# Earlier loads in the branch projections, and splits, loads and sums dealt anew around W_o, its norms and the first gate pair

## The chip, the cores and the metric

The kernel runs on one core of a Trainium2 chip. The time is that of one execution on the device, in microseconds (us), as the median of several runs. The engines are called PE (TensorE, matrix products), DVE (VectorE), ACT (ScalarE), POOL (GpSimd) and SP (SyncE, which issues most of the DMA transfers).

## The reference, cut to what matters

One layer of a decoder for a prompt of 1024 tokens and 8 single tokens of other sequences (1032 columns in all), with 1024 channels in float32:

```python
h = _rmsnorm(x, lp['norm1_w']) * (1 + sc1) + sh1
qkv, gdn_gate, beta_raw, a_raw, sq, sk, sv, ga, gb = _split_in(h @ lp['w_in'])
...
y_a = _gdn_out(o_a, gdn_gate, lp['gdn_onorm_w']) @ lp['w_gdn_out']
...
y_b = o_b @ lp['w_swa_out']
mix = (jax.nn.sigmoid(ga) * y_a + jax.nn.sigmoid(gb) * y_b) @ lp['w_o']
x = x + gt1 * mix
h2 = _rmsnorm(x, lp['norm2_w']) * (1 + sc2) + sh2
gate = h2 @ lp['w_ffn_gate']
up = h2 @ lp['w_ffn_up']
...
gc = _causal_dwconv(gate_ext, lp['ffn_conv_w'], L) + lp['ffn_conv_b']
x = x + gt2 * ((jax.nn.silu(gc) * up) @ lp['w_ffn_down'])
```

The part that is touched here begins with the two output projections of the branches, `w_swa_out` and `w_gdn_out`, goes on with `w_o` and the second norm, and ends in the first pair of blocks of `w_ffn_gate`.

## The kernel before

Every product of float32 matrices is made of three matmuls of rounded numbers. An operand x is split into a high part, x rounded by ACT (`split`, L129), and a low part, x minus the high part, made on DVE (L130); `mm3` adds high by high (L180), low by high (L181) and high by low (L182). A weight or an activation is ready for PE when both engines are done with it; the first of the three matmuls needs only the high parts. A block of 128 output channels takes 24 matmuls for each group of columns.

The work is kept transposed, channels on the 128 partitions and tokens along the free axis. In the branches the tokens are cut into three parts (`PARTS`: t = 0, 1 of 384 columns, t = 2 of 264), from W_o on into four quarters (`QUARTERS`, q = 0 to 3, of 256 to 260).

`branches` (L1332) first runs y_b: for each block j of 128 channels of `w_swa_out` the product of `ob`, times its gate (`yb_out`). While it does so, `oa` and the part of y_b that was parked in DRAM (`ub`) are loaded, at j = 3 and 4 (L1364). Then it runs y_a with `w_gdn_out`: `ya_out` (L1343) multiplies by the gate, adds y_b and splits the sum into the operands of W_o, `self.mix` (tiles `bmh`, `bml`). Beside these products stands the recurrence of the 8 single tokens (`sample_delta`), whose states go through DRAM (`dlr`) into `b1l`, are scaled by ACT (L1216) and updated by DVE.

`output_pass` (L1407) makes quarter q of W_o: for each j the weight (`output_weights`, only at q = 0, with three `raw` buffers), the residual x from DRAM (`xT`, L1431), the product, the addition on DVE (L1472) and the square for the norm; the sum is also written to `x1d`. The room of x is that of operands of the last branch product, so its loads can start only once that product is done. `second_norm` (L1479) sums the squares on PE, takes the power -1/2 on POOL (`power`, L125), spreads the factors with a diagonal `dg` (DVE, L1505) and a matmul (PE, L1506), and scales.

The feed-forward products run in a form in which a pair of blocks takes seven products in place of eight: `operands` makes sums and differences of the columns (tiles `bmh`, `pk`, differences in `td`), `pair_weights` (L1577) those of the weights (`ws`, on POOL for `w_ffn_gate`), and `ffn_gate_up` runs the pair.

The code gives streams of instructions with priorities (`weave`); a scheduler, which models the time of each instruction, puts each engine's instructions in one order, and each engine takes them strictly in that order. `issue_after` keeps what follows behind a given instruction. Since SP is one such engine, a transfer that waits for its room holds back all behind it.

Of the kernel before, what the change touches and what calls it, by code (L numbers as in the profile page):

```python
# [64 lines left out]
class Step:  # L65
# [57 lines left out]
    def power(self, out, in_, expo):  # L123
        e = expo[:in_.shape[0], :]
        self.nc.gpsimd.tensor_tensor(out, in_, e.broadcast_to(list(in_.shape)), op=ALU.pow)  # L125

    def split(self, hi, lo, x, eng=None):

        self.nc.scalar.activation(hi, x, AF.Copy)  # L129
        (eng or self.nc.vector).tensor_tensor(lo, x, hi.bitcast(F32), op=ALU.subtract)  # L130
# [1201 lines left out]
    def branches(self, pool, pool2):  # L1332
# [10 lines left out]
        def ya_out(t, ps):  # L1343
            u, v = ub[t][:, j, :], gate(self.sga, j, t)
            nc.vector.tensor_tensor(v, ps, v, op=ALU.mult)
            nc.vector.tensor_tensor(u, u, v, op=ALU.add)
            r0, n = PARTS[t]
            for q, (lo, m) in enumerate(QUARTERS):
                c, e = max(lo, r0), min(lo + m, r0 + n)
                if c < e:  # L1350
                    self.split(*(x[:, j, c - lo:e - lo] for x in self.mix[q]), u[:, c - r0:e - r0])
# [4 lines left out]
        for j, t in (*late[:2], *((j, t) for j in range(7) for t in (0, 1) if t or (j, t) in late[2:]), (7, 1), *late[-1:] * (7 not in EARLY)):  # L1356
# [7 lines left out]
            if t and j in (3, 4):  # L1364
                with self.tc.issue_after(self.w_load.ins):
                    if j == 3:
# [40 lines left out]
    def output_pass(self, pool, q):  # L1407
# [5 lines left out]
        def add(t, ps):  # L1413
            self.add_gated(t, ps, j, 16)
            sq = self.t(pool, [P, QW], "nsq" if j else "nss", bufs=2)[:, :n]
            if q == 3 and j > 4:
                nc.vector.tensor_tensor(sq, x1[:, j, :], x1[:, j, :], op=ALU.mult)
            else:
                nc.scalar.activation(sq, x1[:, j, :], AF.Square)
# [8 lines left out]
        for j in range(8):  # L1428
            if q == 0:
                self.wo.append(self.output_weights(j))  # L1430
            nc.sync.dma_start(x1[:, j, :], self.xT[j][:, lo:lo + n])  # L1431
# [12 lines left out]
    def output_weights(self, j):  # L1444
# [9 lines left out]
        for c in (0, 512) if j == 0 else (slice(None),):  # L1454
            c = c if j else slice(c, c + 512)
            self.split(*(x[:, c] for x in w), raw[:, c])
# [22 lines left out]
    def second_norm(self, pool, psum, t):  # L1479
# [22 lines left out]
        self.power(rs[:, :nc_], rs[:, :nc_], self.mhalf)  # L1502
# [18 lines left out]
    def operands(self, pool, p, stage):  # L1521
# [21 lines left out]
        self.split(*ops[2], d)  # L1543
        yield
        minus(b1, b2, b1)
        self.split(*ops[4], b1)
        yield
        minus(a2, a2, d)
        self.split(*ops[5], a2)
        yield  # L1550
        self.split(*ops[6], b2)
# [25 lines left out]
    def pair_weights(self, pool, w, f, eng=None):  # L1577
# [20 lines left out]
        out = [put(a0), put(b0)]  # L1598
        s1 = calc(a1, b1, ALU.add)
# [53 lines left out]
    def ffn_gate_up(self, pool, pool2, psum, f, w, first):  # L1653
# [9 lines left out]
        def gate(p, i, q, ps, r):  # L1663
            lo, n = QUARTERS[2 * p + q]
            zq = z[i][:, 2 + lo:2 + lo + n]
            if r is None:
                nc.scalar.copy(zq, ps)
            else:
                nc.vector.tensor_tensor(zq, ps, r, op=ALU.add)
# [25 lines left out]
        w = self.pair_weights(pool, I["w_ffn_up"][0], f, nc.vector if first else None)  # L1695
# [213 lines left out]
    def second_half(self):  # L1909

        nc, S = self.nc, ExitStack
        with S() as c:
# [6 lines left out]
            with S() as right:  # L1919
                xr = self.pool("xr", 1, ctx=right, side="right")  # L1920
                with S() as left:
# [3 lines left out]
                    self.squares, self.X, self.wo = {}, {}, []  # L1925
# [151 lines left out]
```

## Time and profile before

| | |
|---|---|
| runs | 2074.53, 2076.88, 2081.3 us, median 2076.88 |
| profiled execution | 2076.01 us |
| its span in the profile | 2074.3 us |
| PE busy | 2008.0 us, 97% of the span |
| DVE, ACT, POOL busy | 1356.4, 902.5, 522.1 us |
| moved by DMA | 275.75 MB, 133 GB/s over the span |

A profile row gives the start in us from the span's beginning, the duration, engine and line of the kernel (a helper's line where one records the operation), the output and inputs by their tile names, and in brackets how long the engine had been idle before it and what released it. SPq rows are transfers that SP issues: their duration is that of the issue. PE rows of one form overlap, so that the step from start to start tells the speed. Stretches of time show, for each engine, busy time, then the granted clock of PE, the mean use of the DMA engines and the bytes moved.

### The profile page before, as it was taken

Reading aid. Unit: us, or ns where it says so; the run is one execution under the profiler, and the core shown is the slowest. Engines: PE = TensorE matmul, PEld = TensorE weight load, DVE = VectorE, ACT = ScalarE, POOL = GpSimd, SP = SyncE. Lnnn points to the kernel's source line nnn. Section 1 sums busy time; section 2 is a strip of 40 time slices with the busy share of each in tenths; the row PEclk is TensorE's granted clock in tenths of the full one; section 3 lists DMA queues with packets and bytes.
Section 4 is the critical chain, followed back from the end, with each engine's and each line's share of the span. In section 5 each row is a group of like instructions: output and inputs, shape, how many; then the busy total and the mean of one; then the engine's idle time right before and its main releaser. Section 6 shows DMA issues by size and latency. Waiting matters only on the chain.

```text
span 2074.3 us, 41298 instructions
## 1 busy us (share of the span) xinstructions
PE 2008.0 (97%) x16245; PEld 1905.2 (92%) x16245; DVE 1356.4 (65%) x2714; ACT 902.5 (44%) x2233; POOL 522.1 (25%) x594
## 2 busy tenths in 40 slices
PE   7999999999999999989989999999999999999998
PEld 4987877799999999979989999999999999999997
DVE  4755767483655746656554575479886777668866
ACT  4664545443334343442442452345544444444443
POOL 2000000131321211211111000004556556543561
PEclk9999999999999999999999999999999999999999
DMA  8256443332322322312276774513333332388783
GB/s 293 72 145 207 138 168 116 96 99 65 82 82 57 77 69 52 91 37 61 67 198 184 253 231 133 146 58 90 105 98 103 107 95 91 126 280 280 265 285 115
DMA packets 301887, 275.75 MB, mean 133 GB/s; under 512 B 59730, under 2 KB 248111, under 8 KB 301676
## 3 DMA queue, kind: packets, MB, share of 16 engines
q1 hardware_dynamic: 295642, 252.14, 39.7%
q0 software_dynamic: 5552, 20.37, 2.8%
q8 instruction: 127, 2.08, 0.4%
q14 instruction: 68, 0.56, 0.1%
q10 hardware_dynamic: 498, 0.61, 0.1%
HBM read 212.93 MB, written 62.51 MB: 133 GB/s over the span
## 4 chain that ended last, share of the span: by engine, by line
PE 82%; DMA 6%; DVE 6%; ACT 3%; issue 1%; SPq 1%; POOL 0%; DVEq 0%; POOLq 0%; ACTq 0%
PE mm L180 18%; PE mm L181 18%; PE mm L182 18%; PE wv L180 3%; PE wv L182 3%; PE wv L181 3%; PE wy L182 2%; PE wy L180 2%; PE wy L181 2%; PE pv L652 1%; DMA raw<-in_w_swa_out_dram 1%; PE pt L190 1%; PE tp L190 1%; PE mm L264 1%; PE sc L614 1%
## 5 line engine op out<-in xcount | busy, mean ns | idle before, releaser
L180 PE MATMUL mm<-b1h,wh 128*128 128x384 f32 (+1 forms) x1520 | 496.9, 328 | 4.0 <-ACT gt L1294 1.6
L181 PE MATMUL mm<-b1l,wh 128*128 128x384 f32 (+1 forms) x1520 | 489.1, 323 | 0.0
L182 PE MATMUL mm<-b1h,wl 128*128 128x384 f32 (+1 forms) x1520 | 487.7, 323 | 0.4 <-DVE wl L130 0.3
L180 PEld LDWEIGHTS mm<-b1h,wh 128*128 128x128 f32 x1520 | 286.5, 189 | 13.1 <-issue 4.6
L181 PEld LDWEIGHTS mm<-b1l,wh 128*128 128x128 f32 x1520 | 286.8, 189 | 4.4 <-issue 4.0
L182 PEld LDWEIGHTS mm<-b1h,wl 128*128 128x128 f32 x1520 | 286.0, 188 | 4.5 <-issue 2.8
L129 ACT ACTIVATE wh<-raw 128x1024 fp32r<-128x1024 f32 x83 | 87.1, 1050 | 124.4 <-PE mm L181 72.0
L130 DVE TENSOR_TENSOR wl<-raw,wh 128x1024 fp32r<-128x1024 f32 x82 | 101.9, 1244 | 59.8 <-ACT wh L129 58.9
L181 PE MATMUL mm<-pk,w 128*128 128x260 f32 (+1 forms) x440 | 124.3, 283 | 1.1 <-DVE pk L130 1.1
L180 PE MATMUL mm<-pk,w 128*128 128x260 f32 (+1 forms) x440 | 124.3, 283 | 0.0
L182 PE MATMUL mm<-pk,w 128*128 128x260 f32 (+1 forms) x440 | 124.1, 282 | 0.0
L130 DVE TENSOR_TENSOR w<-ws,w 128x512 fp32r<-128x512 f32 x88 | 78.2, 890 | 36.0 <-ACT w L129 35.8
L1626 ACT COPY bml<-mm 128x256 f32<-128x256 f32 (+1 forms) x132 | 48.9, 371 | 97.6 <-PE mm L182 94.5
L180 PE MATMUL mm<-bmh,w 128*128 128x260 f32 (+1 forms) x320 | 90.3, 282 | 0.0
L182 PE MATMUL mm<-bmh,w 128*128 128x260 f32 (+1 forms) x320 | 90.1, 282 | 0.0
L1681 DVE SCALAR_TENSOR_TENSOR fa<-fz,fcw,fa 128x512 f32<-128x512 f32 x88 | 74.5, 867 | 18.1 <-ACT fa L1679 17.8
L180 PE MATMUL mm<-b2h,wh 128*128 128x384 f32 (+1 forms) x256 | 83.2, 328 | 3.0 <-ACT wh L129 2.9
L181 PEld LDWEIGHTS mm<-pk,w 128*128 128x128 f32 x440 | 82.8, 188 | 1.3 <-DVE pk L130 1.3
L181 PE MATMUL mm<-b2l,wh 128*128 128x384 f32 (+1 forms) x256 | 83.6, 327 | 0.4 <-DVE b2l L130 0.4
L180 PEld LDWEIGHTS mm<-pk,w 128*128 128x128 f32 x440 | 82.9, 188 | 0.2 <-ACT bml L1626 0.2
L182 PEld LDWEIGHTS mm<-pk,w 128*128 128x128 f32 x440 | 82.9, 189 | 0.0
L182 PE MATMUL mm<-b2h,wl 128*128 128x384 f32 (+1 forms) x256 | 82.9, 326 | 0.0
(645 smaller groups left out, 5889.9 us busy)
## 6 DMA issues: line engine op xcount, KB each, us to landing
raw<-in_w_in_dram SPq DMA_DIRECT2D x59, 512.0 KB
ws<-in_w_ffn_down_dram SPq DMA_DIRECT2D x55, 256.0 KB
raw<-xd SPq DMA_DIRECT2D x47, 258.0 KB
raw<-in_w_ffn_down_dram SPq DMA_DIRECT2D x47, 256.0 KB
raw<-in_w_ffn_gate_dram SPq DMA_DIRECT2D x22, 512.0 KB
raw<-in_w_ffn_up_dram SPq DMA_DIRECT2D x22, 512.0 KB
qst<-in_w_mod_dram SPq DMA_DIRECT2D x16, 512.0 KB
raw<-in_w_mod_dram SPq DMA_DIRECT2D x16, 512.0 KB
```

What stands on the lines that cost most here:

```text
L129: self.nc.scalar.activation(hi, x, AF.Copy)
L130: (eng or self.nc.vector).tensor_tensor(lo, x, hi.bitcast(F32), op=ALU.subtract)
L180: mm(ps, whi, xhi, start=first, stop=False, **kw)
L181: mm(ps, whi, xlo, start=False, stop=False, **kw)
L182: self.last_mm = mm(ps, wlo, xhi, start=False, stop=last, **kw).ins
L190: self.nc.tensor.transpose(out, in_, self.ident[:p, :p])
L264: nc.tensor.matmul(ps[32 * j:32 * j + 32], self.cT[:, k0 + j, :], ws[j // 2][:, j % 2, :], start=k0 == 0, stop=k0 > 0)
L614: self.scored = nc.tensor.matmul(sc[:, r, 256 - w:256], q, KH[:, lo:lo + w], start=True, stop=False)
L652: nc.tensor.matmul(pv[64 * r:64 * r + 64], V[:, n - back, ch], ps[:, r::2, :], start=back == 0, stop=back == (n > 0))
L1626: self.last_copy = nc.scalar.copy(r[p, i], x[p])
L1681: nc.vector.scalar_tensor_tensor(ai[:, c:e], zi[:, j + c:j + e], col(j), ai[:, c:e], op0=ALU.mult, op1=ALU.add)
```

## The change

1. In `branches` the loads of `oa` part 0 and of `ub` are placed at j = 1 and 2 in place of 3 and 4.
2. `ya_out` of the last part (t = 2) for j = 6 and 7 rounds the high parts on DVE, as an addition that writes the rounded type, and no more on ACT.
3. The residual x for W_o is loaded two blocks of channels at a time: 16 transfers in place of 32.
4. The low parts of the weights j = 0 and 1 of W_o are made on POOL in place of DVE.
5. The sums of the first weight of `w_ffn_gate` are issued behind the power of the norm of quarter 1.
6. In the first gate pair, the first copy out of PSUM is DVE's in place of ACT's, the additions of its first half are issued behind the last square, and the splits of the operands and of one weight behind the split of the third operand.

```diff
     def split(self, hi, lo, x, eng=None):
-        self.nc.scalar.activation(hi, x, AF.Copy)
-        (eng or self.nc.vector).tensor_tensor(lo, x, hi.bitcast(F32), op=ALU.subtract)
+        return (self.nc.scalar.activation(hi, x, AF.Copy),
+                (eng or self.nc.vector).tensor_tensor(lo, x, hi.bitcast(F32), op=ALU.subtract))
+    def behind(self, made):
+        stack = ExitStack()
+        for x in made:
+            stack.enter_context(self.tc.issue_after(x.ins))
+        return stack
...
+            if t < 2 or j < 6:
+                nc.vector.tensor_tensor(u, u, v, op=ALU.add)
+                for rooms, a, b, m in spans:
+                    self.split(*(x[:, j, a:a + m] for x in rooms), u[:, b:b + m])
+                return
+            for (hi, _), a, b, m in spans:
+                nc.vector.tensor_tensor(hi[:, j, a:a + m], u[:, b:b + m], v[:, b:b + m], op=ALU.add)
             nc.vector.tensor_tensor(u, u, v, op=ALU.add)
+            for (hi, lo), a, b, m in spans:
+                nc.vector.tensor_tensor(lo[:, j, a:a + m], u[:, b:b + m], hi[:, j, a:a + m].bitcast(F32), op=ALU.subtract)
...
-            if t and j in (3, 4):
+            if t and j in (1, 2):
                 with self.tc.issue_after(self.w_load.ins):
-                    if j == 3:
+                    if j == 1:
                         oa = {0: self.load_part(pool2, self.oa, 0, rooms=first)}
...
-            nc.sync.dma_start(x1[:, j, :], self.xT[j][:, lo:lo + n])
+            if j % 2 == 0:
+                nc.sync.dma_start(x1[:, j:j + 2, :], self.xT[j:j + 2, :, lo:lo + n].rearrange("k p n -> p k n"))
...
-            self.split(*(x[:, c] for x in w), raw[:, c])
+            self.split(*(x[:, c] for x in w), raw[:, c], None if j > 1 else self.nc.gpsimd)
...
-        self.power(rs[:, :nc_], rs[:, :nc_], self.mhalf)
+        self.factors.append(self.power(rs[:, :nc_], rs[:, :nc_], self.mhalf))
...
-        self.split(*ops[2], d)
+        made = self.split(*ops[2], d)
         yield
-        minus(b1, b2, b1)
-        self.split(*ops[4], b1)
+        self.third = made if p else ()
+        with self.behind(self.third):
+            minus(b1, b2, b1)
+            self.split(*ops[4], b1)
...
-        out = [put(a0), put(b0)]
-        s1 = calc(a1, b1, ALU.add)
+        out = [put(a0)]
+        with self.behind(after):
+            out.append(put(b0))
+        with self.behind(self.factors[1:2] if f == 0 and len(self.factors) == 3 else ()):
+            s1 = calc(a1, b1, ALU.add)
...
-                nc.scalar.copy(zq, ps)
+                (nc.vector.tensor_copy if first and not p else nc.scalar.copy)(zq, ps)
```

How the orders change at the three places of which the prediction speaks most. SP at the start of W_o, before: `raw` are the weights of W_o (the first three of eight stand ahead of these rows), `x` the residual.

```order
L1448 DMA raw_14410<-in_w_o_dram 128x8x128
L1431 DMA x_2196_14333<-xT_950 128x256 x6
L1448 DMA raw_14447<-in_w_o_dram 128x8x128
L1431 DMA x_2196_14333<-xT_950 128x256 x3
L1448 DMA raw_14483<-in_w_o_dram 128x8x128
L1431 DMA x_2196_14333<-xT_950 128x256 x2
L1448 DMA raw_14519<-in_w_o_dram 128x8x128
```

And SP there with the change:

```order
L1464 DMA raw_14409<-in_w_o_dram 128x8x128
L1447 DMA x_2196_14333<-xT_950 128x2x256 x8
L1464 DMA raw_14446<-in_w_o_dram 128x8x128
L1447 DMA x_2197_14334<-xT_950 128x2x260 x4
L1464 DMA raw_14481<-in_w_o_dram 128x8x128
L1464 DMA raw_14517<-in_w_o_dram 128x8x128
```

Weight 3 stands behind eight transfers of two blocks in place of six of one, weight 4 behind four more of two blocks in place of three of one.

SP where the second weight of W_gdn_out is loaded, before: `oa` is the other operand, whose remaining parts are loaded into `b2l`, `dlr` the states of the recurrence, `sga` a gate.

```order
L135 DMA raw_13464<-in_w_gdn_out_dram 128x8x128
L1250 DMA b2l_2110_13423<-oa_927 128x2x256 x2
L1393 DMA gt_13419<-sgb_2613 128x384
L1250 DMA b2l_2110_13423<-oa_927 128x2x256 x2
L1214 DMA b1l_2052_12734<-dlr_13089 128x1024
L1393 DMA gt_13501<-sga_2614 128x384
L1214 DMA b1l_2052_12734<-dlr_13089 128x1024
L135 DMA raw_13470<-in_w_gdn_out_dram 128x8x128
L1250 DMA b2l_2112_13439<-oa_927 128x2x384 x4
```

And with the change:

```order
L142 DMA raw_13464<-in_w_gdn_out_dram 128x8x128
L1221 DMA b1l_2052_12734<-dlr_13089 128x1024
L1408 DMA gt_13419<-sgb_2613 128x384
L1257 DMA b2l_2110_13423<-oa_927 128x2x256 x3
L1221 DMA b1l_2052_12734<-dlr_13089 128x1024
L1257 DMA b2l_2110_13423<-oa_927 128x2x256
L1408 DMA gt_13501<-sga_2614 128x384
L1221 DMA b1l_2052_12734<-dlr_13089 128x1024
L1257 DMA b2l_2112_13439<-oa_927 128x2x384 x4
L142 DMA raw_13470<-in_w_gdn_out_dram 128x8x128
```

The states' loads have moved up, and the second weight (`raw_13470`) has gone from ahead of the last four `oa` loads to behind them. On PE the second product of W_gdn_out is now that of those four loads; before it came after those of the second weight and of part 2.

POOL at the second norm, before: `rs` are the powers of the norms of quarters 0 and 1, `ws` the sums of the first gate weight.

```order
L1589 TENSOR_TENSOR ws_15523<-raw_15513,raw_15515 128x512
L1589 TENSOR_TENSOR ws_15525<-ws_15523,raw_15513 128x512
L1589 TENSOR_TENSOR ws_15533<-raw_15513 128x512
L125 TENSOR_TENSOR rs_15396<-rs_15396,mhalf 128x2
L125 TENSOR_TENSOR rs_15431<-rs_15431,mhalf 128x2
```

And with the change:

```order
L130 TENSOR_TENSOR w_2201_14339<-raw_14336,w_2200_14338 128x512 x2
L130 TENSOR_TENSOR pk_2205_14376<-raw_14374,pk_2205_14376 128x1024
L125 TENSOR_TENSOR rs_15380<-rs_15380,mhalf 128x2
L125 TENSOR_TENSOR rs_15415<-rs_15415,mhalf 128x2
L1609 TENSOR_TENSOR ws_15507<-raw_15497,raw_15499 128x512
L1609 TENSOR_TENSOR ws_15509<-ws_15507,raw_15497 128x512
L1609 TENSOR_TENSOR ws_15517<-raw_15497 128x512
```

The low parts of W_o's first two weights are new on POOL, and both powers have moved ahead of the sums.

29 lines of the change are left out of this document (15 added, 14 removed).

## The prediction

> **What bounds the kernel now.** Read in this order: the page's busy times, whom TensorE (PE) waited for, PE's timeline at the longest of those waits, then the other engines and SP's DMA issues (SPq) there. The page first:
>
> ```profile
> PE 2008.0 (97%) x16245; PEld 1905.2 (92%) x16245; DVE 1356.4 (65%) x2714; ACT 902.5 (44%) x2233; POOL 522.1 (25%) x594
> ```
>
> PE is busy for 97% of the span, so the change, which leaves every product as it is, can only win PE's waits, and the time a low clock costs behind them. PE's waits from 1100 to 1440 us, the stretch that the edits touch (total, times, longest):
>
> ```profile
> core 0 of [0], span 2074.3 us
> engine line waited for: us in total, times, longest us
> PE nr L1506 <- DVE dg L1505: 3.0, 1, 3.0
> PE mm L180 <- ACT wh L129: 2.9, 1, 2.9
> PE mm L1439 <- ACT w L129: 2.1, 1, 2.1
> PE wv L180 <- ACT w L129: 1.1, 1, 1.1
> PE mm L181 <- DVE pk L130: 1.1, 1, 1.1
> ```
>
> The places, in order of time: **A**, the second W_gdn_out weight (2.9); **B**, the start of W_o (2.1); **C**, the norm of quarter 0 (3.0); **D**, the first gate pair (1.1 and 1.1). PE's own timeline (start, duration, instruction, idle before):
>
> ```profile
> 1195.54 0.44 PE L180 MATMUL mm<-b2h,wh 128*128 128x384 f32 x1 [2.88 <-ACT wh L129]
> ...
> 1196.36 0.38 PE L180 MATMUL mm<-b2h,wh 128*128 128x264 f32 x1
> ...
> 1199.62 0.38 PE L180 MATMUL mm<-b2h,wh 128*128 128x264 f32 x1
> ```
> ```profile
> 1285.02 0.49 PE L1439 MATMUL mm<-bmh,w 128*128 128x256 f32 x1 [2.06 <-ACT w L129]
> ...
> 1288.52 1.13 PE L1439 MATMUL mm<-bmh,w 128*128 128x256 f32 x8
> 1289.48 0.28 PE L180 MATMUL mm<-bmh,pk 128*128 128x256 f32 x1
> ```
> ```profile
> 1324.54 0.70 PE L1506 MATMUL nr<-dg,ones 128*128 128x256 f32 x2 [3.05 <-DVE dg L1505]
> ...
> 1325.20 0.28 PE L182 MATMUL mm<-bmh,pk 128*128 128x256 f32 x1
> ...
> 1326.38 0.28 PE L180 MATMUL mm<-bmh,pk 128*128 128x256 f32 x1
> ```
>
> At B, 8 matmuls take 0.96 us from 1288.52 (0.12 each), but the 16 before them 3.50 us: a low clock, costing 3.50 - 16 x 0.12 = 1.6. At A the 15 steps from 1196.36 to 1199.62 take 3.26, where 0.12 each would be 1.8: 1.5 more. At C the 10 steps behind the wait take 1.18, so no loss. A thus cost 2.9 + 1.5 = 4.4, B 2.1 + 1.6 = 3.7, C 3.0, D 2.2: 13.3 us at most to win, 0.64% of the run.
>
> **The change, part by part.** *A: the earlier loads.* DMA use of two stretches (last columns: clock, DMA share, GB/s), and rows of ACT and DVE:
>
> ```profile
> 1142.00:1157.00 15.00, 15.00 (x153) 14.26 (x146) 5.58 (x14) 3.16 (x6) 0.00 (x0) 1.00 0.39 112
> 1157.00:1172.00 15.00, 14.91 (x87) 14.05 (x86) 8.73 (x15) 6.06 (x8) 0.00 (x0) 1.00 0.97 306
> ```
> ```profile
> 1192.09 2.45 ACT L1216 ACTIVATE b1l<-b1l,kq 128x128 f32<-128x128 f32 x8 [1.24 <-DMA b1l<-dlr]
> 1194.45 1.04 ACT L129 ACTIVATE wh<-raw 128x1024 fp32r<-128x1024 f32 x1
> ```
> ```profile
> 1196.66 0.55 DVE L1345 TENSOR_TENSOR gt<-mm,gt 128x384 f32<-128x384 f32 x1
> 1197.13 0.95 DVE L130 TENSOR_TENSOR b2l<-b2l,b2h 128x768 fp32r<-128x768 f32 x1
> ```
>
> The weight that PE waited for at 1195.54 was rounded only after eight scalings that themselves waited for a load (1.24 idle): a late DMA in a full queue. The moved transfers hold 4 x 0.39 MB (oa) and 1.08 + 2 x 0.20 MB (ub), 3.05 MB together; 1142 to 1157 has (306 - 112) x 15 = 2.9 MB to spare (306 being the next stretch's rate), so nearly all of it leaves the full stretch, and the scalings' loads come earlier. But in the new order the second raw weight is issued behind the four loads of the other oa part instead of ahead, and PE's second tile is now that part's. DVE there makes its gate product (0.55, once PE has ended the first tile) and a low part (0.95) before PE can go on: 1.5 us of wait is built in, and I add 0.4 for the load ahead of it, an allowance between none and the whole of the old wait. A wait of 1.9, in pieces, leaves the clock as at C: 4.4 - 1.9 = **2.5 won**, between 0 (loads as late as now) and 2.9 (1.5 alone). What pays for it: the W_swa weights issued behind the moved loads; PE hardly waits at present, and the new loads end before 1157, so I take nothing.
>
> The Trainium skill's page "TensorE: Matmul & The Clock Gate" (Part 1) has the clock fall to half after an idle window of about 3.4 us. By it none of the waits above would be punished, and by it A would win 1.0 in place of 2.5. The trace disagrees: 2.06 and 2.88 us of idle were followed by matmuls at nearly half speed.
>
> *B: W_o.* SP's and ACT's rows, the low part on DVE, and the DMA's rates:
>
> ```profile
> 1283.00 2.71 SPq L1431 DMA_DIRECT2D x<-xT  x6
> 1286.35 0.39 SPq L1448 DMA_DIRECT2D raw<-in_w_o_dram  x1
> ```
> ```profile
> 1284.36 1.14 ACT L129 ACTIVATE w<-raw 128x512 fp32r<-128x512 f32 x2
> ...
> 1291.49 1.06 ACT L129 ACTIVATE pk<-raw 128x1024 fp32r<-128x1024 f32 x1 [0.81 <-DMA raw<-in_w_o_dram]
> ```
> ```profile
> 1292.59 1.23 DVE L130 TENSOR_TENSOR pk<-raw,pk 128x1024 fp32r<-128x1024 f32 x1 [2.42 <-ACT pk L129]
> ```
> ```profile
> 1286.00:1290.00 4.00, 4.00 (x26) 4.00 (x26) 3.00 (x4) 1.39 (x2) 0.00 (x0) 0.68 0.87 249
> 1290.00:1296.00 6.00, 6.00 (x54) 6.00 (x53) 2.33 (x4) 2.85 (x4) 0.00 (x0) 1.00 1.07 306
> ```
>
> In ACT's queue the first weight's high part (1284.36) stands behind the split of the last branch tile; with that split on DVE, ACT is free and the weight is rounded before W_a ends (1285.02 - 2.06 = 1282.96). The low parts on GpSimd, about 1.3 us per 512 columns by the sums under C, end in time. So W_o starts 2.1 sooner and at full clock: 3.7 won. Now what is late next. Weight 3's raw load is issued behind six x loads of 0.13 MB (1283.00, then 1286.35); now it is behind eight of 0.26 MB: 2.10 MB instead of 0.79, on a queue that is full (249, then 306 GB/s). Before, x and weight, 1.31 MB, took from 1283.00 to ACT's start at 1291.49. After, 1.31 MB more at 306 is 4.3 us: 1295.8. The other end is 306 for all 2.62 MB from the first issue on (1283.4): 1292.0. I take the middle, 1294.0, having a row for neither. PE asks for it after three weights, 72 matmuls, at 1282.96 + 72 x 0.12 = 1291.6. High part: 1294.0 + 1.06 = 1295.1, a wait of 3.5; the low part 1.23 later costs 1.0 more. Weight 4 comes behind 4 x 0.27 MB more, 1.59 MB with its own, 5.2 us at 306, against 3.0 between the two askings and low parts: 2.2. Weight 6, behind 1.33 MB more, by the same reckoning 0.9. Sum 7.6 (from 4.6, 1292.0 and no wait for weight 6, to 9.4). A low clock behind the first of these waits costs nothing more, as it takes from the next. Even were weight 3 as early as before (1291.49 + 1.06), PE would wait 1.0 + 1.0 for it, so B wins 1.7 at best. Taken: 3.7 - 7.6 = **3.9 lost** (from 1.7 won to 5.7 lost).
>
> *C: the power ahead of the sums.* GpSimd (POOL) and DVE:
>
> ```profile
> 1322.08 1.26 POOL L1589 TENSOR_TENSOR ws<-raw 128x512 f32<-128x512 f32 x1
> 1323.30 0.73 POOL L125 TENSOR_TENSOR rs<-rs,mhalf 128x2 f32<-128x2 f32 x1
> ```
> ```profile
> 1315.64 0.16 DVE L1501 TENSOR_SCALAR rs<-nr 128x2 f32<-128x2 f32 x1 [2.42 <-PE nr L1496]
> ```
>
> The power's input was there at 1315.80; it ran at 1323.30, right behind the last of three sums of a weight. Now both powers stand ahead: 1315.8 + 0.73 + 0.43 for dg, about 1317.0, long before PE needs it (1321.5). The sums wait for the second power, that of quarter 1, too; their weights are used only in the gate pair, behind all of W_o but its last norm. **3.0 won**, 2.5 at least.
>
> *D: the first gate pair.*
>
> ```profile
> 1400.00:1440.00 40.00, 36.70 (x295) 35.52 (x295) 39.62 (x56) 24.33 (x44) 15.09 (x15) 1.00 0.25 77
> ```
>
> DVE (third busy column) is busy 39.62 of 40 us and loses nothing here: a copy comes to it from ACT and no work goes. The low parts PE waited for are made sooner, but PE's work of the pair's earlier products moved behind them, so PE asks for them sooner too. **0**, from 1.5 lost to 2.2 won (both waits gone).
>
> Sum: 2.5 - 3.9 + 3.0 + 0 = 1.6 faster. The profiled execution took 2076.01 (span 2074.3 and 1.7 around it), 0.9 under the median of the runs, 2076.88; 1.6 taken from the median gives 2075.3. About 0.3%, 6.2 us, is what a measurement can tell from no change: below 2070.7 is faster, above 2083.1 slower.
>
> **The rivals.** *1. The double loads don't hold the weight back.* For it: weight 3 was in place at 1291.49 although x loads filled the queue, and a 0.26 MB load may move better than two of half of it. Then B wins its best 1.7: 2.5 + 1.7 + 3.0 = 7.2, 2069.7; with D's and A's best up to 9.8, 2067. Against it: the queue is full already and SP issues in order. The Trainium skill's "DMA: Bandwidth & Descriptors" (Rules for kernel authors) asks for large transfers, 1 MiB and up, for bandwidth, which would favour this rival; no run here shows the double loads yet. Chance 0.28.
>
> *2. Slower: W_o is fed at the rate of its start.* If x and weights move at 220 GB/s, below the 249 of the row from 1286, weight 3 is there 1.31 / 0.22 = 6.0 us later than before, 1297.5, and the waits become 6.9 + 1.0 for it, 4.3 for weight 4 and 4.0 for weight 6: 16.2. B then loses 12.5, and the sum is 7.0 slower, 2083.9. It decides from about 225 GB/s down. Against it: 306 in the row that follows. Chance 0.12.
>
> *3. Nothing goes but C.* The earlier loads let A's weight come no sooner, since it now stands behind four more loads, and B gives back just what it won: 2076.9 - 3.0 = 2073.9. Chance 0.12, within 0.3%. My forecast, 2071 to 2080, has 0.48.
>
> Faster 0.28, same 0.60, slower 0.12. The range from rival 1's 2067 to short of rival 2: 2067 to 2082.
>
> **What would show it.** A: PE's wait for ACT wh gone, short waits for b2l in its place. B: no wait at W_o's first matmul and no low clock; a wait of 2 to 6 us for weight 3 (DMA raw, then ACT pk) about 8.6 us later, and a shorter one for weight 4. C: POOL's power right behind DVE's rs, and no wait at nr. D: PE's waits from 1400 to 1440 together 1 to 4 us. I am wrong if weight 3 is rounded before PE asks for it, or if PE waits in W_swa for a weight behind the moved loads.

## The result and the profile after

The changed kernel took 2086.98 us, the median of 15 runs (2080.47 to 2095.15), against 2078.11 of the kernel before (15 runs, 2071.17 to 2087.9). The ratio is 1.0043, with an interval from 1.0033 to 1.0054: slower by about 9 us, where 1.6 faster was forecast, and outside the range. The profiled execution of the changed kernel took 2080.47 us (span 2078.8) and was the fastest of its 15. A second profile of the same kernel, taken later, had a span of 2083.4. Both are used below.

The page's busy times, after:

```profile
PE 2011.6 (97%) x16245; PEld 1908.8 (92%) x16245; DVE 1359.0 (65%) x2716; ACT 901.5 (43%) x2228; POOL 522.9 (25%) x597
```

PE issues the same 16,245 matmuls and is busy 3.6 us longer for them. The two longest of PE's waits from 1100 to 1450 us, after:

```profile
PE mm L187 <- ACT b2h L129: 3.5, 1, 3.5
PE mm L189 <- DVE w L130: 2.3, 1, 2.3
```

The helper's three matmul lines are now L187 to L189. The waits at `nr` (C) and at W_o's first matmul (B) are gone. In their place stand a longer wait at A, for another tile, one of 2.3 for a weight's low part, and several of under 1 us for W_o's later weights.

Since both kernels issue the same number of matmuls, the start of the N-th one can be compared. It is worked out from PE's records; the columns after the first time are differences to the kernel before, in us:

| N | place | before | after | after, second profile |
|---|---|---|---|---|
| 8800 | ahead of A | 1135.14 | -0.22 | -0.56 |
| 9700 | behind A, in W_gdn_out | 1270.42 | +2.22 | +4.34 |
| 10100 | behind W_o's norm (B and C) | 1327.08 | +2.45 | +4.72 |
| 10300 | ahead of D | 1350.92 | +2.44 | +4.71 |
| 11000 | behind D | 1439.09 | +4.07 | +6.36 |
| 16244 | the last | 2066.20 | +4.05 | +8.71 |

So A lost 2.4 (second profile 4.9). B and C together lost 0.2 (0.4). The matmuls around D lost 1.6 in both. The stretch that was touched thus lost 4.3 (6.9) of the 9 us.

**A, after.** PE, then ACT, then SP:

```profile
1195.87 0.69 PE L187 MATMUL mm<-b2h,wh 128*128 128x384 f32 x1 [3.55 <-ACT b2h L129]
1197.10 0.69 PE L188 MATMUL mm<-b2l,wh 128*128 128x384 f32 x1 [0.54 <-DVE b2l L130]
1197.58 0.53 PE L189 MATMUL mm<-b2h,wl 128*128 128x384 f32 x1
1197.90 0.53 PE L187 MATMUL mm<-b2h,wh 128*128 128x384 f32 x1
...
1202.60 0.33 PE L187 MATMUL mm<-b2h,wh 128*128 128x384 f32 x1
1202.77 0.33 PE L188 MATMUL mm<-b2l,wh 128*128 128x384 f32 x1
```
```profile
1175.54 4.80 ACT L1223 ACTIVATE b1l<-b1l,kq 128x128 f32<-128x128 f32 x16 [2.14 <-DMA b1l<-dlr]
```
```profile
1182.93 2.45 ACT L1223 ACTIVATE b1l<-b1l,kq 128x128 f32<-128x128 f32 x8 [2.59 <-DMA b1l<-dlr]
...
1185.43 1.05 ACT L129 ACTIVATE wh<-raw 128x1024 fp32r<-128x1024 f32 x1
...
1192.63 2.44 ACT L1223 ACTIVATE b1l<-b1l,kq 128x128 f32<-128x128 f32 x8 [0.22 <-DMA b1l<-dlr]
1194.99 3.11 ACT L129 ACTIVATE b2h<-b2l 128x768 fp32r<-128x768 f32 x4
```
```profile
1186.10 0.33 SPq L1221 DMA_DIRECT2D b1l<-dlr  x1
1186.53 2.06 SPq L1257 DMA_DIRECT2D b2l<-oa  x4
1189.43 0.37 SPq L142 DMA_DIRECT2D raw<-in_w_gdn_out_dram  x1
```

The steps from start to start are 0.32 from 1197.58 on and 0.17 from 1202.60: PE waited 3.55 + 0.54, in two pieces, and was then at half speed for about 5 us. By the granted clock the half-speed stretch at A lasts 6.83 us, against 3.41 before: 1.7 us more lost, beside 1.2 more of waiting, together a little above the 2.4. What PE waits for, the high part of the last oa part, stands in ACT's queue behind eight scalings whose states were loaded at 1186.10. That load goes out when DVE has ended the updates that read its room, those of the eight scalings of 1182.93:

```profile
1184.69 1.39 DVE L1224 SCALAR_TENSOR_TENSOR b1h<-b1h,egb,b1l 128x128 f32<-128x128 f32 x5
```

Before, the states' load was issued at 1184.08 and the second weight's at 1186.39, now at 1189.43. SP and ACT, before:

```profile
1184.08 0.45 SPq L1214 DMA_DIRECT2D b1l<-dlr  x1
1186.39 0.38 SPq L135 DMA_DIRECT2D raw<-in_w_gdn_out_dram  x1
```
```profile
1184.06 1.04 ACT L129 ACTIVATE wh<-raw 128x1024 fp32r<-128x1024 f32 x1
```

The forecast had the states earlier. The first W_gdn_out weight, too, is rounded later (1185.43, before 1184.06): 24 scalings stand ahead of it now (16 from 1175.54, 8 from 1182.93), 16 before.

Did the stretch become emptier? Windows of before, then of after (last columns: clock, DMA share, GB/s):

```profile
1180.00:1190.00 10.00, 10.00 (x59) 10.00 (x58) 9.38 (x26) 7.80 (x22) 1.85 (x2) 1.00 1.04 356
```
```profile
1142.00:1157.00 15.00, 15.00 (x146) 14.32 (x139) 9.12 (x18) 6.55 (x10) 0.00 (x0) 1.00 0.96 312
1157.00:1172.00 15.00, 14.99 (x88) 14.32 (x86) 5.02 (x10) 2.65 (x4) 0.55 (x1) 1.00 0.51 154
...
1180.00:1190.00 10.00, 10.00 (x59) 10.00 (x58) 7.76 (x22) 6.11 (x17) 1.78 (x2) 1.00 0.99 336
```

The bytes moved as forecast: 1142 to 1157 is full now, and 1157 to 1172 fell from a share of 0.97 to 0.51. But the stretch in which the states and the second weight travel, from 1180 on, is about as full as it was (0.99 in place of 1.04).

**B, after.** PE, POOL, DVE, SP and ACT:

```profile
1290.87 0.39 PE L189 MATMUL mm<-bmh,w 128*128 128x256 f32 x1 [2.31 <-DVE w L130]
```
```profile
1281.84 2.81 POOL L130 TENSOR_TENSOR w<-raw,w 128x512 fp32r<-128x512 f32 x2 [0.42 <-ACT w L129]
1284.61 2.62 POOL L130 TENSOR_TENSOR pk<-raw,pk 128x1024 fp32r<-128x1024 f32 x1
```
```profile
1283.54 1.41 DVE L1364 TENSOR_TENSOR t<-t,sgx 128x264 f32<-128x264 f32 x1
1284.97 2.62 DVE L1366 TENSOR_TENSOR bml<-t,bmh 128x4 fp32r<-128x4 f32 x2
...
1288.51 0.43 DVE L1364 TENSOR_TENSOR t<-t,sgx 128x264 f32<-128x264 f32 x1
1288.97 0.50 DVE L1366 TENSOR_TENSOR bml<-t,bmh 128x4 fp32r<-128x4 f32 x2
...
1289.59 1.23 DVE L130 TENSOR_TENSOR w<-raw,w 128x1024 fp32r<-128x1024 f32 x1
```
```profile
1285.23 4.18 SPq L1447 DMA_DIRECT2D x<-xT  x8
```
```profile
1296.06 1.06 ACT L129 ACTIVATE pk<-raw 128x1024 fp32r<-128x1024 f32 x1 [4.35 <-DMA raw<-in_w_o_dram]
```

While POOL makes its new low parts (1281.84 to 1287.23), DVE's additions and subtractions for the last branch blocks take 1.41 and 2.62 us in place of 0.43 and 0.50 for the same instructions five microseconds later. So DVE gets to the third weight's low part only at 1289.59, and PE waits 2.31 for it. The fourth weight (weight 3) is rounded at 1296.06, 10.8 us after the first x load was issued; PE, held up by the earlier wait, then asks late enough to wait only 0.34, and 0.73, 0.76 and 0.25 for what follows.

**C, after.** The power runs 0.08 us behind its input (DVE's `rs` ends at 1322.71 + 0.16), with POOL idle for 35.71 us before it, and PE does not wait at `nr`:

```profile
1322.95 0.73 POOL L125 TENSOR_TENSOR rs<-rs,mhalf 128x2 f32<-128x2 f32 x1 [35.71 <-DVE rs L1517]
```

**D.** PE's waits from 1400 to 1445 us add up to 4.1 after (1.0, 1.0, 0.6, 0.6, 0.5, 0.4), against 3.2 before (1.1, 1.1, 0.7, 0.3). In the second profile they are 2.2, but with a granted clock of 0.96 from 1400 to 1440.

### The profile page after: what moved, and what is told of

It is laid out like the page before. It is cut to its first block, busy times and chain, and to the rows that moved or that the text cites. A ratio compares the mean times of both kernels' runs of the same rounds, so it can differ in the third digit from the quotient of the medians.

```text
span 2078.8 us, 41283 instructions
## 1 busy us (share of the span) xinstructions
PE 2011.6 (97%) x16245; PEld 1908.8 (92%) x16245; DVE 1359.0 (65%) x2716; ACT 901.5 (43%) x2228; POOL 522.9 (25%) x597
## 4 chain that ended last, share of the span: by engine, by line
PE 84%; DVE 6%; DMA 5%; ACT 3%; issue 1%; SPq 1%; POOL 0%; DVEq 0%; POOLq 0%; ACTq 0%
PE mm L187 19%; PE mm L188 18%; PE mm L189 18%; PE wv L187 3%; PE wv L189 3%; PE wv L188 3%; PE wy L189 2%; PE wy L187 2%; PE wy L188 2%; PE pv L659 1%; DMA raw<-in_w_swa_out_dram 1%; PE pt L197 1%; PE tp L197 1%; PE mm L271 1%; DMA b1l<-dlr 1%
## 5 line engine op out<-in xcount | busy, mean ns | idle before, releaser
L187 PE MATMUL mm<-b1h,wh 128*128 128x384 f32 (+1 forms) x1520 | 497.4, 329 | 3.5 <-ACT gt L1301 1.6
L189 PE MATMUL mm<-b1h,wl 128*128 128x384 f32 (+1 forms) x1520 | 488.5, 324 | 0.3 <-DVE wl L130 0.3
L187 PEld LDWEIGHTS mm<-b1h,wh 128*128 128x128 f32 x1520 | 287.0, 189 | 12.5 <-issue 4.6
L189 PEld LDWEIGHTS mm<-b1h,wl 128*128 128x128 f32 x1520 | 286.6, 189 | 4.2 <-issue 2.8
L187 PE MATMUL mm<-pk,w 128*128 128x260 f32 (+1 forms) x440 | 124.5, 283 | 1.5 <-ACT pk L129 1.0
L189 PE MATMUL mm<-pk,w 128*128 128x260 f32 (+1 forms) x440 | 124.1, 282 | 0.0
L189 PE MATMUL mm<-bmh,w 128*128 128x260 f32 (+1 forms) x320 | 90.5, 283 | 2.3 <-DVE w L130 2.3
L187 PE MATMUL mm<-bmh,w 128*128 128x260 f32 (+1 forms) x320 | 90.7, 283 | 0.6 <-DVE fa L1727 0.6
L187 PE MATMUL mm<-b2h,wh 128*128 128x384 f32 (+1 forms) x256 | 83.7, 329 | 3.5 <-ACT b2h L129 3.5
L187 PEld LDWEIGHTS mm<-pk,w 128*128 128x128 f32 x440 | 82.9, 188 | 1.9 <-ACT pk L129 1.2
L189 PE MATMUL mm<-b2h,wl 128*128 128x384 f32 (+1 forms) x256 | 83.6, 328 | 0.0
L189 PEld LDWEIGHTS mm<-pk,w 128*128 128x128 f32 x440 | 82.9, 189 | 0.0
```

The costliest lines, as they stand in the source:

```text
L187: mm(ps, whi, xhi, start=first, stop=False, **kw)
L189: self.last_mm = mm(ps, wlo, xhi, start=False, stop=last, **kw).ins
```

## The experiments

The theory after the result: A loses because, with the loads early, ACT and SP take up the states of the recurrence ahead of the projection's own operands (edit 1); B's waits come from the contention of POOL and DVE (edit 4) or from the double x loads (edit 3). The rival: an edit that moves no wait, or the clock alone, makes the difference. Each ratio is to the kernel before on the same chip, with its interval; "before + " and "after - " name the edits by their numbers in the section on the change.

A single trace is one sample. PE's first wait at A was 2.7 to 4.8 us in six kernels that leave the loads as they were (the kernel before, after - edit 1, those with edit 3, 4 or 5 alone, and the one with W_o's weights first), and 3.6 to 5.4 in the six traces with edit 1 in its own order. From matmul 8800 to 9700 the first six differ from the kernel before by -0.6 to 2.5 us (0.7 on average), the others by 2.4 to 4.9 (3.7). The wait at C was 3.0 in the kernel before, but 0 to 2.4 (1.3 on average) in the seven other kernels without edit 5. One of them, before + edit 4:

```profile
PE nr L1521 <- DVE dg L1520: 0.7, 1, 0.7
```

The five other kernels that leave B and C alone take 0.6 to 1.3 us less than the kernel before from matmul 9700 to 10100. A difference of one or two us between two traces thus shows nothing by itself. Nor is an edit ever quite alone, since the scheduler orders the instructions anew for each kernel.

### A: which part of the earlier loads costs

**Before + edit 1.**

```diff
-            if t and j in (3, 4):
+            if t and j in (1, 2):
```


> The kernel before with edit 1 alone (the oa and ub loads at j = 1 and 2). My theory, 'three places': the change lost time at A because PE's second product of W_gdn_out became the one of the last loaded oa part, whose roundings stand in ACT's queue behind the scalings of the recurrence; that comes with the moved loads, so this kernel shows PE waiting 3 to 4 us for ACT b2h there and is 2 to 4 us slower than the kernel before (2080 to 2082), its W_o as before. The rival, 'W_o only': the earlier loads are good or neutral and all that was lost was lost from W_o on; then this kernel is as fast as the one before or up to 2.5 us faster.

Measured 1.0044 [1.0029, 1.0059]. PE waited 4.58 for ACT's b2h and 0.68 for the low part. The loads alone lose as much as the whole change, where 2 to 4 us were expected.

**After - edit 1.** The other way about:

> The changed kernel with edit 1 undone: the loads at j = 3 and 4, and with them the former order of products and of the scalings. From the traces so far the places cost, against the kernel before: A 2.8 (mean of six kernels with early loads), B 3.3, C -3.0, D 1.1, together 4.2; measured were 8.9. Theory 'loads and clock': the part not found in the traces belongs to the long waits at A, which more often cost a second half-clock stretch in the timed runs; then without edit 1 the ratio is 1.000 to 1.001 (B, C and D alone: 1.4 us). The rival 'W_o and after': edits 3 to 6 cost more than the traces show; then the ratio stays at 1.002 or above.

1.0020 [1.0008, 1.0032]; A waits 3.2, near before's 2.9. On the same chip the changed kernel once more:

> The changed kernel once more, beside the one without edit 1 on the same chip, for a second trace of it: the ratio should again be 1.003 to 1.005. If its trace loses at A and B what the first lost (2.4 and 3.3) and the span is nearer to the median, the rest lies in half-clock stretches elsewhere, which differ from execution to execution; if A or B lose 3 us more than in the first trace, the rest lies there.

1.0042 [1.0028, 1.0056]. By these two the earlier loads cost 0.0022 x 2078 = 4.6 us, half of the loss, and the five other edits the rest together; by the run with edit 1 alone they cost all of it. Each of these ratios is uncertain by 2.5 to 3 us to either side, so the share of edit 1 is somewhere from half of the loss to the whole. A ratio of 1.002 is what the rival had forecast, not the theory.

**Edit 1 with PE's former order.** The last oa part is loaded behind the second weight again:

```diff
-        oa[1] = self.load_part(pool2, self.oa, 1)
...
+            if j0 == 0:
+                with self.tc.issue_after(self.w_load.ins):
+                    oa[1] = self.load_part(pool2, self.oa, 1)
```


> Edit 1 alone, but the last oa part is loaded behind the second W_gdn_out weight again, which gives PE back its former order of products there. 'Three places': the early loads were harmless and the order did the harm, so the wait for ACT b2h goes; the second weight's scalings-and-weight chain on ACT is some 3 us earlier than before, PE waits 0 to 1.5 us there in place of 2.9, and the time is 2 to 4 us below the kernel before. The rival: if the transfers themselves crowd the weights of W_swa and W_gdn_out, PE still waits 2 us or more at that place and nothing is won.

1.0022 [1.0009, 1.0035]: about 4.6 us less than with edit 1 alone, but no gain in PE's wait at A, against what was expected. DVE, SP and PE:

```profile
1188.09 1.22 DVE L130 TENSOR_TENSOR wl<-raw,wh 128x1024 fp32r<-128x1024 f32 x1 [0.31 <-ACT wh L129]
```
```profile
1189.34 0.38 SPq L142 DMA_DIRECT2D raw<-in_w_gdn_out_dram  x1
```
```profile
1198.11 0.69 PE L187 MATMUL mm<-b2h,wh 128*128 128x384 f32 x1 [4.61 <-ACT wh L129]
```

The order of the two products was only part of it. The second weight's load is issued the moment the first weight's low part is done (1188.09 + 1.22 = 1189.31), since it takes the same `raw` room. Before, the same two times were 1186.36 and 1186.39. So whatever delays the first weight's split delays the second weight's load; here 24 scalings stand ahead of that split on ACT.

**The scalings ahead of the second weight.** In both of the next, with the former order of products, the last heads' scalings wait for that weight's split (`hold` stops the stream at head h):

```diff
+            if h == 4:                # with edit 1;  h == 3 without
+                yield "hold"
...
+        with self.behind(self.w_made[:1]):
+            for _ in samples:
+                pass
```


> Edit 1 alone with the former order of products, and the state work of the heads from the fifth on (load, scalings, update) behind the high part of the second W_gdn_out weight. In the kernel before, 32 scalings of the recurrence stand ahead of that weight's high part in ACT's queue; with the early loads it is 40, and PE waited 4.6 us there. Theory 'scalings': that block of eight (2.5 us and its load's landing) is the whole loss at A; with it behind, PE's wait falls below 1.5 us, no half-clock stretch follows, and the time is 2 to 4 us below the kernel before (2073 to 2075). The rival 'full queue': the weight's own load or the operands' loads are late anyway; the wait stays above 2.5 us and the time stays 3 us or more above the kernel before.

With edit 1: 1.0018 [1.0004, 1.0032], a wait of 5.16: the theory fell. ACT:

```profile
1197.19 1.06 ACT L129 ACTIVATE wh<-raw 128x1024 fp32r<-128x1024 f32 x1 [2.75 <-DMA raw<-in_w_gdn_out_dram]
```

ACT stood idle for 2.75 us, with no scaling ahead: the weight had not landed.

> The kernel before, loads where they were, with the state work of the heads from the fourth on behind the high part of the second W_gdn_out weight: 24 scalings ahead of it in place of 32. 'Scalings': PE's 2.9 us wait for ACT wh at A falls below 1 us and its half-clock stretch goes: 2.5 to 4.5 us below the kernel before. 'Full queue': the weight has not landed any sooner, the wait stays at 2 us or more and the time within 1.5 us of the kernel before.

Without edit 1: 1.0004 [0.9988, 1.0019]; the wait stays at 2.66, with the weight again late by DMA (ACT idle for it 3.98). So the scalings directly ahead of that weight do not set the wait. Its load was issued at 1188.56 and 1183.99 here, each time 0.03 after the end of the first weight's low part.

**The first weight ahead.** Edit 1 with the former order, the third head's scalings behind the first weight's split, and the fourth head's load behind that of the second weight:

```diff
+            if h in (2, 3):
+                yield "hold"
...
+        with self.behind(made[:1]):
+            next(samples)
+        with self.tc.issue_after(self.w_load.ins):
+            for _ in samples:
+                pass
```


> Edit 1 alone, the former order of products, and two things put back in their place: the third head's scalings behind the high part of the first W_gdn_out weight, and the fourth head's load behind the load of the second weight. Theory 'buffer': a weight's raw buffer is needed for the weight after next; with the early loads 24 scalings instead of 16 stand ahead of the first weight's split, so the buffer came free 3 us later (the second weight's load was issued at 1189.3 against 1186.4), and its 8 us of flight ended 4.6 to 5.2 us after PE asked. Then here the second weight's load is issued 3 us or more before 1186, PE's wait there falls below 2 us, and the time is at most that of the kernel before (2 us below to 1 above). The rival 'full queue': whatever is issued first, the bytes of 1175 to 1200 take as long; the wait stays above 3.5 us and the time 3 us or more above the kernel before.

1.0002 [0.9991, 1.0014]: the loss of the earlier loads is gone. DVE, SP and PE:

```profile
1185.26 1.23 DVE L130 TENSOR_TENSOR wl<-raw,wh 128x1024 fp32r<-128x1024 f32 x1 [0.26 <-ACT wh L129]
```
```profile
1187.74 0.41 SPq L142 DMA_DIRECT2D raw<-in_w_gdn_out_dram  x1
```
```profile
1196.02 0.45 PE L187 MATMUL mm<-b2h,wh 128*128 128x384 f32 x1 [0.51 <-ACT wh L129]
```

With the first weight's room free at 1186.49 the second one's load goes out at 1187.74, PE waits 0.51 in place of 4.6, and the next matmuls run at full speed. In time from the span's start the load is only 1.6 us earlier than with edit 1 in the former order (1189.34), and not the 3 us ahead of 1186 that were expected; but PE asks 2.0 later in this trace (1195.51 against 1193.50), so that against PE's asking the load is 3.6 ahead. Two things were put back at once, the scalings and the fourth head's load; which of them does it was not separated.

### B: contention or the double loads

**After - edit 4** (`None if j > 1 else self.nc.gpsimd` taken out again):

> The changed kernel with edit 4 undone: the low parts of the first two W_o weights on DVE again. 'Three places': beside those two GpSimd instructions a DVE subtraction of 264 columns took 1.41 us where it takes 0.43 alone, and two tiny ones 2.62, so that the third W_o weight's low part came 3 us late; with them on DVE these rows take 0.4 to 0.5, PE's 2.3 us wait for that low part falls below 0.7, and the time is 2 to 4 us below the changed kernel (2083 to 2085). The rival, 'transfers': W_o waits for weight 3 behind the x loads whatever DVE does; the 2.3 us reappear as a wait for ACT pk or DVE pk of weight 3 and the time stays within 1 us of the changed kernel (2086 to 2088).

1.0028 [1.0016, 1.0040]. DVE's rows, and PE's waits from 1278 to 1340 us:

```profile
1285.56 0.43 DVE L1364 TENSOR_TENSOR t<-t,sgx 128x264 f32<-128x264 f32 x1
1286.03 0.50 DVE L1366 TENSOR_TENSOR bml<-t,bmh 128x4 fp32r<-128x4 f32 x2
```
```profile
PE mm L189 <- DVE pk L130: 1.7, 3, 0.8
PE mm L187 <- ACT pk L129: 1.6, 1, 1.6
PE mm L1455 <- DVE w L130: 1.0, 1, 1.0
PE mm L187 <- DVE x L1488: 0.6, 1, 0.6
```

The stretched rows are back at 0.43 and 0.50, so POOL's work had stretched them. But the waits only move: 4.9 in sum, against 4.4 in the changed kernel. Behind the low part stands weight 3, late by the double loads. The ratio is 0.0015 below the changed kernel's, with intervals that overlap.

**Before + edit 4**, where DVE has nothing to do beside POOL's first two low parts:

> The kernel before with edit 4 alone (low parts of W_o's first two weights on GpSimd, three instructions). From the contention seen in the changed kernel: DVE's instructions that run beside them are stretched by 1 to 2 us each or the GpSimd ones are (2.6 in place of 1.3 per 512 columns), the weights' low parts arrive 2 us later, and W_o is 1 to 3 us slower than before. The rival: DVE has little to do at that place in this kernel, so nothing is stretched and the time stays within 1 us.

0.9992 [0.9976, 1.0007]: no difference, where 1 to 3 us slower were expected. POOL's two of 512 columns took 2.52, and that of 1024 columns took 3.40 where a DVE low part of 1024 columns (1.24) began 0.13 ahead of it.

**After - edit 3** (single x loads):

> The changed kernel with edit 3 undone: x loaded one block at a time. 'Transfers': weight 3's raw load stands behind six small x loads again and is used by ACT about 5 to 6 us behind the first x load's issue and not 10.8; PE's waits for ACT pk and DVE pk of weights 3 to 7 (2.1 us in the changed kernel) go, and 1 to 3 us are won against the changed kernel (2084 to 2086). The rival: the wait for the third weight's low part (2.3 us, GpSimd and DVE) bounds this place alone; then nothing changes, 2087.

1.0018 [1.0003, 1.0032]. Weight 3, on ACT:

```profile
1293.16 1.06 ACT L129 ACTIVATE pk<-raw 128x1024 fp32r<-128x1024 f32 x1 [2.49 <-DMA raw<-in_w_o_dram]
```

It stands behind eight single loads here and is rounded 9.0 us after the first of them was issued (1284.18), against 10.8 behind eight double ones. From matmul 9700 to 10100 this trace gains 2.5, where the changed kernel lost 0.2. Of these 2.8, 1.0 are waits (3.4 in sum, the 2.3 for the third weight's low part still among them), and 1.7 the half-speed stretch behind that wait, which this trace does not have. The ratio is 0.0025 below the changed kernel's 1.0043, about 5 us.

**Before + edit 3:**

> The kernel before with edit 3 alone (x in 16 loads of two blocks). Its W_o still starts 2 us late, so that weight 3 is wanted 3.6 us later than in the changed kernel; it stands behind six double loads here, 0.79 MB more than before, which is 2.6 us at 306 GB/s against 1.3 us of slack in the kernel before (low part at 1293.8, wanted at 1295.1). So PE waits 1 to 3 us for weights 3 and 4 and the time is 0 to 3 us above the kernel before. If double loads move better than single ones, there is no wait and the time is the same or less.

1.0006 [0.9994, 1.0018]. W_o starts 2.1 late there, as before, and weight 3 is on hand when ACT comes to it (no DMA wait); PE waits only 0.2 for its low part. So the double loads cost hardly anything by themselves. By the run above they cost together with the earlier start of W_o.

**Before + edits 2 and 5, with the weights of W_o ahead of the x loads:**

```diff
-            if q == 0:
-                self.wo.append(self.output_weights(j))
-            nc.sync.dma_start(x1[:, j, :], self.xT[j][:, lo:lo + n])
+            if q == 0 and j in (0, 4, 5, 6, 7):
+                self.wo += [self.output_weights(i) for i in (range(4) if j == 0 else (j,))]
+            with self.tc.issue_after(self.wo_load.ins) if q < 4 else nullcontext():
+                nc.sync.dma_start(x1[:, j, :], self.xT[j][:, lo:lo + n])
```


> The kernel before with edits 2 and 5 (the last branch tile's rounding on DVE, the power ahead of the sums) and, in place of edits 3 and 4, the loads of x issued behind those of the W_o weights 3 to 7. If W_o's weights are held back by the x loads, here W_o starts without its 2.1 us wait, keeps the full clock and waits for no weight: 3.7 at W_o and up to 3.0 at the norm, so 4 to 7 us below the kernel before. The rival: x arrives too late then, and DVE's additions, which want it, hold up the PSUM buffers or the norm; then PE waits 2 us or more behind W_o's first products and the gain is under 3.

0.9992 [0.9981, 1.0003]. The longest of PE's waits from 1278 to 1340 us, with 0.4 and 0.2 behind it:

```profile
PE mm L1455 <- DVE w L130: 1.0, 1, 1.0
```

From matmul 9700 to 10100 this trace gains 4.4 us: in the trace the early start of W_o is worth having once weight 3 does not queue behind x. The total, 1.7 us lower with an interval up to 0.6 higher, does not resolve it.

### C, D and all together

**Before + edit 5:**

> The kernel before with edit 5 alone (the sums of the first gate weight behind the power of quarter 1). Its order differs from the kernel before in a handful of rows only. Both theories: PE's wait for dg, 3.0 us, goes and nothing comes in its place: 2.5 to 3 us below the kernel before (2075). If the time does not move, a wait further on takes it back and my term C was no gain at all.

0.9995 [0.9981, 1.0009]. The only wait left in W_o's stretch is that of its start, 2.1; the matmuls 9700 to 10100 gain 3.4 in the trace (the kernels that leave B and C alone gain up to 1.3 there), and again the total does not resolve so little.

**After - edit 6:**

> The changed kernel with edit 6 undone (the first gate pair's copies, splits and sums as before). From the traces: PE's waits from 1400 to 1445 us are 4.2 us in the changed kernel and 3.2 in the one before, so 0 to 1.5 us below the changed kernel; a larger gain would mean that edit 6 costs something the two traces do not show.

1.0064 [1.0047, 1.0081]. D's waits are those of before again (1.1, 1.1, 0.7, 0.3), and matmuls 10300 to 11000 take 0.5 longer than before. The median gains nothing by it; it is rather higher than the changed kernel's, with intervals that overlap. Nor do the traces tie the 1.6 us to edit 6: over these matmuls the eleven kernels that leave it out differ from the kernel before by 0.0 to 2.8 us, the five traces with it by 0.3 to 1.9.

**Edit 1 with the first weight ahead, edits 2 and 5, and W_o's weights ahead of x** (the two changes shown above, together):

> The two before put together: the early loads with the first weight ahead of the scalings, edits 2 and 5, and W_o's weights ahead of x. If the places are independent, its time below the kernel before is the sum of the two, 4 to 9 us. If the full DMA queue ties them, it is no better than the one with W_o's weights first.

2073.1 against 2076.34 us, 0.9983 [0.9974, 0.9993]: 3.2 us less than the kernel before, under the 4 to 9 that were expected. The trace has no half-speed stretch from 1100 to 1460 us. PE's waits from 1278 to 1340 us:

```profile
PE mm L1472 <- DVE w L130: 1.0, 1, 1.0
PE mm L189 <- DVE pk L130: 0.9, 2, 0.8
```

## Why the prediction was wrong, point by point

**A is the step that failed.** It reads "so nearly all of it leaves the full stretch, and the scalings' loads come earlier", which with the sum behind it was to win 2.5. The first half held in the windows (0.97 to 0.51). The second didn't: the states' last load went out 2.0 us later and the second weight 3.0 later, in a stretch that was as full as before, and A lost 2.4 (4.9 in the second profile). What the prediction took for a slow transfer in a full queue was in good part a late issue. With PE's former order the second weight's load goes out only when the first weight has left its room, and that one is rounded behind the recurrence's scalings, of which the early loads bring in eight more; in the changed kernel's own order the wait is for the oa part behind the last eight scalings, whose load was late in the same way. From its issue to its use that weight takes 6.7 to 9.7 us in the eleven kernels with the former order (8.1 in the kernel before), so the transfer itself varies as well. Nor did PE's wait stay short: of the 1.5 us that were "built in" on DVE 0.54 appeared, but 3.55 for ACT stood ahead of it, and where the prediction has the wait leave "the clock as at C" half speed lasted 6.83 us. The wait of 2.9 that was to be won was besides one sample of 2.7 to 4.8. The lower bound of A, "loads as late as now", left out that they could come later. Rival 3 named the place ("stands behind four more loads") but put A's loss at nothing. The runs that undid it are the one with the first weight ahead (1.0002) against that with edit 1 alone (1.0044). One small term was put at nothing wrongly, too: behind the moved loads PE waits for a W_swa weight in most traces with edit 1, 0.65 + 0.29 in the second profile from 1162.10 and 1.16 + 0.30 in the last experiment, though not in the first profile; no kernel without edit 1 shows it.

**B's size held, in part by luck.** 3.9 lost was forecast; in the traces 0.2 (0.4) for B and C together, less the 3.0 that C won, makes 3.2 to 3.4 lost. Weight 3 came 10.8 us after the first x load, where the middle taken from two ends meant 11.0 (1294.0 - 1283.0). But its long wait was not seen: another, 2.3 for the third weight's low part, stood ahead of it and hid it. Of the 7.6 us of waits in the forecast's sum 2.1 came; that wait of 2.3, and the half-speed stretch of 3.41 us behind it, are not in that sum. "The low parts on GpSimd ... end in time" held for those two weights and missed what POOL does to DVE meanwhile. Rival 1, double loads that don't hold the weight back, fell; rival 2's rate did not come about (its 225 GB/s or less; the windows from 1286 and 1290 moved 275 and 333).

**C held in its mechanism**: the wait went, as the power's row and the run with edit 5 alone show. The size, "3.0 won, 2.5 at least", was that of one execution: the seven other kernels with the sums ahead of the power waited 1.3 on average. In the median of many runs C was thus worth rather 1.3 than 3.0, an estimate from those seven waits, which would explain 1.7 us of what the forecast lacks.

**D was put at 0.** The matmuls around it lost 1.6 in the two traces, just beyond the 1.5 of its worse end, but no run ties this to edit 6.

Sum of the prediction's steps as measured: 2.4 + 3.3 - 3.0 + 1.6 = 4.3 slower (6.9 in the second profile), where 1.6 faster was forecast. A alone makes 4.9 to 7.4 of the miss. The other 2 to 5 us of the 9 are not in the touched stretch. The mean granted clock of the timed runs was 0.9891, against 0.9910 for the kernel before beside the first experiments: 0.0019 x 2078 = 3.9 us. But on one and the same chip it was 0.9900 against 0.9907, 1.4 us, for a loss that was as large; and the longer half-speed stretch at A is part of either. The traces show half-speed stretches even where both kernels have the same instructions (from 350 to 365 us the clock was 0.89 after, 1.00 before and in the second profile). How much of them the edits bring about was not settled; edit 2 was run only together with others; and the parts do not add up exactly: after - edit 1 and before + edit 1 together lose 0.0064, the change 0.0043, a gap about as large as the intervals allow.

## What to carry to other kernels

A load that seems late in a full queue may be issued late: before moving other transfers out of its way, find what its issue waits for (here the room that an earlier tile gives back) and what stands ahead of that on the engine that frees it. When a wait at the start of a product is removed, look at the next operand in the queue; a start that is 2 us earlier needs the loads of its fourth weight 2 us earlier too, so weights go ahead of data that is needed later. Judge changes of 0.2% by parts, each against the kernel before on the same chip, and by the same matmul's start in more than two traces, since the clock's own spread is as large and one and the same wait was 0 to 3.0 us here. A wait to be won is better priced by its mean over several traces than by one.

## What the runs showed of the hardware

**POOL stretches DVE.** A DVE addition of 264 columns from two SBUF tiles took 1.41 us in place of 0.43 beside POOL's subtractions. It began at 1283.54 and ended at 1284.95, just behind POOL's end at 1284.65; the next two ended at 1287.59, behind POOL's 1287.23. That reads as waiting for the other engine's instruction to end. The DVE multiplication of the same size from one PSUM and one SBUF tile, at 1282.33 beside the same POOL work, took its usual 0.43. The Trainium skill's page "SBUF — State Buffer" (SBUF: two separate sides) says that of a GpSimd operation and a VectorE operation with two SBUF inputs the first to start has the shared ports for its whole instruction and the other blocks; the rows agree.

**The slow clock's windows.** Slow stretches at A to D last 3.41 or 6.83 us by the records of the granted clock (that behind B's wait from 1291.19 to 1294.60). They follow idle times of 2.06, 2.31 and 2.88 us, though the 3.05 us at C before had none, and one in the second profile (from 1413.05) follows no idle time longer than 1.03. How many fall into one execution varies: the mean granted clock was between 0.986 and 0.995 in the profiles here, which is (1 - 0.986) x 2086 = 29 us against (1 - 0.995) x 2074 = 10. Among the 33 runs of the kernel before beside the first experiments it went from 0.987 to 0.994, 15 us, and their times from 2070.18 to 2083.36, 13 us. The window's length is the one given in the Trainium skill's "TensorE: Matmul & The Clock Gate" (Part 1), 3413 ns; that it takes a whole idle window to lower the clock, which is said there as well, does not agree with these idle times.
